# High and low parts of q and k made by ScalarE and GpSimd instead of GpSimd and VectorE

## The chip, the cores and the metric

The kernel runs on one core of a Trainium2 chip. The metric is the device time of one execution in microseconds (us); the time before is the median of three runs. The engines are TensorE (PE, with its weight loads as PEld), VectorE (DVE), ScalarE (ACT), GpSimd (POOL) and SyncE (SP), whose queue issues the DMAs of this kernel. Each engine works through its own queue in order.

## The reference

One layer of a decoder trunk on 2048 rows of width 1024. Cut to what matters here:

```
h = rms(x) * (1 + scale1(c)) + shift1(c)
u = h @ W_in                       # q, k, v of 8 FoX heads x 64 and of 4 differential heads x (2 x 64)
q = rms(q) * gain_q ; k = rms(k) * gain_k          # per head of 64
FoX:   p = softmax(q k^T / 8 + cumulated log forget gates), causal ; out = p v
diff:  p = softmax(q1 k1^T / 8 + alibi) - lam * softmax(q2 k2^T / 8 + alibi), causal ; out = rms(p v)
x = x + gate1(c) * (concat(FoX, diff) @ W_out)
x = x + gate2(c) * SwiGLU(rms(x) * (1 + scale2(c)) + shift2(c))
```

## The kernel before

All large products are made of fp16 operands that are split in two: a high part (the value rounded to fp16) and a low part (the value minus its high part). A product is then three passes of PE: high by high, high by low, low by high.

The work of the attention half comes in eight groups (four differential, four FoX); a group has 128 columns each of q, k and v. For a group g the in-projection `inproj_pair` (L418) runs over the 16 blocks of 128 rows in eight pairs, so 64 pairs in all. For each block `project` (L424) makes 24 matmuls (L437) into the bank "ip", of which there is one; ScalarE copies q and k out of it (L438) and makes the high part of v (L442), VectorE makes the low part of v (line 443, shown in the trace at the helper's line L144). Then, once for each pair, `split` (L447) squares q and k (L453, ScalarE), sums and takes an inverse root (L455 to L458, and L129 to L135 of the helper), multiplies q and k by it (L459, VectorE, 128x512), multiplies q by the gains (L461, GpSimd, 128x256), and makes the high and the low part of q (a = 0) and of k (a = 1) at L467 and L468, each 128x256. `turn` (L471) has SyncE issue two transposing DMAs of the result (L474) and, after every second pair, four copies (L479, L480) that put it where the score matmuls read it.

The attention walks over units: one unit is 128 keys against up to 512 queries. `scores` (L569) makes two or three matmuls (L579, L580, L582) into one of two banks "st"; ScalarE takes the exponential (L585) and rounds it to the high part (L590); GpSimd makes the low part (L593), with the same operation and types as L468. `weigh` (L596) uses both parts, three units later (PVLAG = 3), in matmuls L607, L608 and L609; L609 is the one that reads the low part. Ahead of a group of units `max_part` (L534) makes the scores once more for the row maxima, into one of three banks "mx" (L546), and VectorE reduces them (L548, L550); `max_row` (L552) gathers the maxima (L555, VectorE; L558, PE; L559, ScalarE). `finish` (L611) scales the outputs (L617 to L639).

The order of the work: `run` (L715) interleaves lists of steps by their weights. The attention of group g runs beside the in-projection of group g + 1 (80% of it; the rest runs in the first units of the group itself), beside the loading and splitting of the next group's weights (`stage_w`, L302), and beside slower side work: the sums of the conditioning over w_ada (`ada_items`, L784, with VectorE's L194, groups 0 to 3), the decay sums (`decay`, group 2), and the scaling of W_out (L821 and L834 on GpSimd, groups 4 and 5). SyncE's queue holds the transposes L474 together with the loads of w_in and w_ada (L312, L327, L791), the writes of the outputs (L666) and others. Which instruction stands where in each engine's queue is settled when the program is built, by a planner that goes by a model of the instructions' times (the last lines of `kernel`). The in-projection is over at about 1375 us; the output projection and the SwiGLU that follow have neither of the two lines.

Of the kernel before, what the change touches and what calls it, by code (L numbers as in the profile page):

```python
# [13 lines left out]
AF = mybir.ActivationFunctionType  # L14
ALU = mybir.AluOpType
# [40 lines left out]
def trunk(ctx, tc, t):  # L56
# [6 lines left out]
    V, A, G, T = nc.vector, nc.scalar, nc.gpsimd, nc.tensor  # L63
# [3 lines left out]
    def bank(tag, dt=F32):  # L67
        n = 512 if dt == F32 else 1024
        return ps.tile([P, n], dt, tag=tag, bufs=PSB[tag], name=f"ps_{tag}")

    def small(n, tag, bufs=3, dt=F32):
        return tiny.tile([P, n], dt, tag=tag, bufs=bufs, name=f"t_{tag}")
# [53 lines left out]
    def rsqrt(v, out, n):  # L126

        l = small(n, f"rl{n}")
        A.activation(l, v, AF.Ln, bias=0.0, scale=1.0)  # L129
        y = small(n, f"ry{n}")  # L130
        A.activation(y, l, AF.Exp, bias=0.0, scale=-0.5)
        q = small(n, f"rq{n}")
        V.scalar_tensor_tensor(out=q, in0=y, scalar=-0.5, in1=y, op0=ALU.mult, op1=ALU.mult)
        V.tensor_tensor(out=q, in0=q, in1=v, op=ALU.mult)
        V.scalar_tensor_tensor(out=out, in0=q, scalar=1.5, in1=y, op0=ALU.add, op1=ALU.mult)  # L135
# [7 lines left out]
    def sub_scaled(out, in_, s, hi):  # L143
        V.scalar_tensor_tensor(out=out, in0=in_, scalar=s, in1=hi, op0=ALU.mult, op1=ALU.subtract)  # L144
# [73 lines left out]
    def next_u():  # L218
        turn["u"] ^= 1
        return uh[:, turn["u"], :]  # L220

    def next_hl():
        turn["h"] ^= 1
        return uh[:, 2 + turn["h"], :].bitcast(F16)
# [124 lines left out]
    def whalf(g, h):  # L349
        return wbuf[:, (2 * g + h) % 3].rearrange("p (k s n) -> p k s n", k=4, s=2)  # L350
# [56 lines left out]
    def xx(mt):  # L407

        return mt[:, 0:2].rearrange("p c n -> p (c n)").rearrange("p (b a n) -> p b a n", b=NB, a=2)

    def vviews(kind, vt):

        if kind == "fox":
            v4 = vt.rearrange("p b (h n) -> p b h n", h=2)
            return v4, HD
        return vt.rearrange("p b (h n) -> p b h n", h=1), 2 * HD

    def inproj_pair(g, res, b0):  # L418

        kind, i = GROUPS[g]  # L420
        N = 392 if g == 0 else 384
        st = {}

        def project(b):  # L424
            if b == 0:
                st["u"] = next_u().rearrange("p (a b n) -> p a b n", a=2, b=2)
            info = res["info"]
            w4 = [whalf(g, h) for h in range(2)]
            blk = b0 + b
            h4 = hts[blk // 4].bitcast(F16).rearrange("p (k s n) -> p k s n", k=KT, s=2)  # L430
            c = (blk % 4) * P
            pt = bank("ip" if g or blk >= 4 * FIRST else PTAGS[blk % len(PTAGS)])
            terms = [(k, n) for k in range(KT) for n in ((0, 0), (0, 1), (1, 0))]
            if g == 0 and blk == 0:
                terms.sort(key=lambda x: x[1])
            for i, (k, (hs, ws)) in enumerate(terms):
                T.matmul(pt[:, 0:N], lhsT=h4[:, k, hs, c : c + P], rhs=w4[k // 4][:, k % 4, ws, 0:N], start=(i == 0), stop=(i == len(terms) - 1))  # L437
            A.activation(st["u"][:, :, b, :], pt[:, 0 : 2 * P].rearrange("p (a n) -> p a n", a=2), AF.Copy, bias=0.0, scale=1.0)  # L438
            v4, W = vviews(kind, res["vt"])
            vs = pt[:, 2 * P : 3 * P].rearrange("p (h n) -> p h n", n=W)  # L440
            hi, lo = v4[:, blk, :, 0:W], v4[:, blk, :, W + 2 : 2 * W + 2]
            A.activation(hi, vs, AF.Copy, bias=0.0, scale=info["dv"])  # L442
            sub_scaled(lo, vs, info["dv"], hi)
            if g == 0:
                V.scalar_tensor_tensor(out=fgl[:, blk * 8 : blk * 8 + 8], in0=pt[:, 384:392], scalar=info["df"], in1=bfr, op0=ALU.mult, op1=ALU.add)

        def split():  # L447
            info, maps = res["info"], res["maps"]
            u = st["u"]
            uf = u.rearrange("p a b n -> p (a b n)")  # L450
            u8 = u.rearrange("p a b (m d) -> p (a b m) d", m=2)
            sq = sqs
            A.activation(sq, uf, AF.Square, bias=0.0, scale=1.0)  # L453
            ss = small(8, "ss")
            V.tensor_reduce(out=ss, in_=sq.rearrange("p (a d) -> p a d", d=HD), op=ALU.add, axis=AX.X)  # L455
            V.scalar_tensor_tensor(out=ss, in0=ss, scalar=1.0 / HD, in1=info["eps8"], op0=ALU.mult, op1=ALU.add)
            r = small(8, "r8")
            rsqrt(ss, r, 8)  # L458
            V.tensor_tensor(out=u8, in0=u8, in1=r.unsqueeze(2).broadcast_to([P, 8, HD]), op=ALU.mult)  # L459
            u4 = u8[:, 0:4]  # L460
            G.tensor_tensor(out=u4, in0=u4, in1=gains[kind].unsqueeze(1).broadcast_to([P, 4, HD]), op=ALU.mult)  # L461
            hl = next_hl().rearrange("p (m b a n) -> p a b m n", m=2, b=2, a=2)
            u3 = u.rearrange("p a b (m d) -> p a b m d", m=2)
            for a in range(2):
                hi = hl[:, a, :, :, 0:HD] if a == 0 else hl[:, a, :, :, HD:P]
                lo = hl[:, a, :, :, HD:P] if a == 0 else hl[:, a, :, :, 0:HD]
                G.tensor_scalar(out=hi, in0=u3[:, a], scalar1=1.0, scalar2=0.0, op0=ALU.mult, op1=ALU.add)  # L467
                V.tensor_tensor(out=lo, in0=u3[:, a], in1=hi, op=ALU.subtract)  # L468
            st["hl"] = hl.rearrange("p a b m n -> p m (b a n)")

        def turn():  # L471
            maps, hl = res["maps"], st["hl"]
            for m in range(2):
                nc.sync.dma_start(xx(maps[m])[:, b0 : b0 + 2].rearrange("p b a n -> p (b a) n"), hl[:, m], transpose=True)  # L474
            if b0 % 4 == 2:
                c0 = (b0 - 2) * P
                for m in range(2):
                    x4 = xx(maps[m])[:, b0 - 2 : b0 + 2]
                    nc.sync.dma_start(maps[m][0:HD, 2, c0 : c0 + QC].rearrange("p (b n) -> p b n", b=4), x4[0:HD, :, 0])  # L479
                    nc.sync.dma_start(maps[m][0:HD, 3, c0 : c0 + QC].rearrange("p (b n) -> p b n", b=4), x4[HD:P, :, 1])  # L480

        return [(1, lambda: project(0)), (1, lambda: project(1)), (0.2, split)], (0.1, turn)

    def decay():
# [820 lines left out]
```

## Time and profile before

| | |
|---|---|
| median of three runs | 2968.4 us (2966.42 to 2976.47) |
| profiled execution, device time | 2964.29 us |
| its span from first to last instruction | 2962.2 us |
| PE busy | 2726.8 us, 92% |
| VectorE busy | 2212.0 us, 75% |
| ScalarE busy | 1410.4 us, 48% |
| GpSimd busy | 1590.5 us, 54% |

Read the table as averages over stages that differ: the in-projection with its attention fills the time up to about 1450 us, the output projection and the SwiGLU the rest. The device time is 2.1 us over the span, for what lies around the first and the last instruction. Below, "waited for" names the instruction that released a waiting one; an engine's idle time costs something only if PE comes to wait for it.

### The profile page before, as it was taken

What the parts mean: (1) busy time and instruction counts of PE and PEld (TensorE: products, weight loads), DVE (VectorE), ACT (ScalarE), POOL (GpSimd) and SP (SyncE); (2) the same over time, 40 slices, a digit from 0 to 9 for tenths busy, and PEclk for the clock granted to TensorE, in tenths of its full rate; (3) what the DMA queues carried; (4) which work ended last, traced back from release to release, by engine and by line L of the source; (5) the groups of instructions that cost most, each with busy time, mean ns of one, the idle gap of its engine ahead of it and who ended that gap; (6) DMA issues with size and microseconds to landing.
All of it is one profiled execution on the core that took longest, in us unless ns stands there. A gap on an engine that the chain in (4) does not pass through costs nothing. (4 is left out here: it accounts for less than half of the span.)

```text
span 2962.2 us, 49590 instructions
## 1 busy us (share of the span) xinstructions
PE 2726.8 (92%) x18902; PEld 1478.2 (50%) x18902; DVE 2212.0 (75%) x4205; ACT 1410.4 (48%) x2597; POOL 1590.5 (54%) x1392
## 2 busy tenths in 40 slices
PE   4899989889898998999989898989989999999998
PEld 3465656556565555665444343434434444444443
DVE  7887786967868687757744887777878688787775
ACT  4566666656666676876552432223322232233231
POOL 3465556655567687765552645544555445444440
PEclk9899999999999999999999999989999999999999
DMA  6322231312223133124776223222234511111101
GB/s 230 80 79 56 62 76 37 84 48 65 70 53 94 46 97 107 44 62 139 182 188 217 86 65 100 65 85 82 89 100 156 171 58 57 57 48 66 57 22 57
DMA packets 269903, 261.93 MB, mean 88 GB/s; under 512 B 204376, under 2 KB 221144, under 8 KB 263904
## 3 DMA queue, kind: packets, MB, share of 16 engines
q1 hardware_dynamic: 269664, 258.75, 29.9%
q8 instruction: 148, 2.42, 0.3%
q14 instruction: 91, 0.75, 0.1%
HBM read 173.55 MB, written 36.91 MB: 71 GB/s over the span
## 5 line engine op out<-in xcount | busy, mean ns | idle before, releaser
L593 POOL TENSOR_TENSOR pxs<-pxs 128x512 f16<-128x512 f32 (+3 forms) x640 | 686.7, 1088 | 344.9 <-ACT pxs L590 180.7
L437 PE MATMUL ps_ip<-wbuf,ht 128*128 128x384 f16 (+1 forms) x2952 | 565.8, 334 | 21.8 <-DVE vts L144 11.0
L1091 PEld LDWEIGHTS <-mt 128*128 128x128 f16 x3696 | 361.1, 98 | 445.8 <-issue 18.4
L1149 PE MATMUL ps_mx<-wide,ht 128*128 128x512 f16 x2112 | 505.1, 382 | 24.2 <-DVE mt L1153 12.1
L585 ACT ACTIVATE pxs<-ps_st,cells 128x512 f32<-128x512 f32 (+3 forms) x640 | 390.9, 620 | 242.8 <-PE ps_st L580 102.6
L1038 POOL TENSOR_TENSOR pxm<-vts 128x512 f32<-128x512 f32 x220 | 296.8, 1376 | 335.2 <-DMA vts<-in_w_gu_dram 308.2
L437 PEld LDWEIGHTS <-ht 128*128 128x128 f16 x3072 | 296.7, 100 | 254.9 <-issue 61.4
L1091 PE MATMUL ps_st<-ht,mt 128*128 128x512 f16 x1584 | 382.1, 384 | 8.4 <-DVE pxm L1099 3.5
L1091 PE MATMUL ps_pv<-ht,mt 128*128 128x512 f16 x1584 | 379.1, 379 | 0.0
L590 ACT ACTIVATE pxs<-pxs 128x512 f16<-128x512 f32 (+3 forms) x640 | 350.9, 565 | 10.1
L1149 PEld LDWEIGHTS <-ht 128*128 128x128 f16 x2112 | 206.5, 99 | 281.1 <-issue 27.9
L607 PE MATMUL ps_pv<-vts,pxs 128*128 128x129 f16 (+1 forms) x2176 | 340.0, 206 | 6.1 <-DVE os L626 6.0
L608 PE MATMUL ps_pv<-vts,pxs 128*128 128x128 f16 (+1 forms) x2176 | 342.3, 208 | 0.0
L609 PE MATMUL ps_pv<-vts,pxs 128*128 128x129 f16 (+1 forms) x2176 | 325.4, 206 | 17.1 <-POOL pxs L593 16.4
L1153 DVE SCALAR_TENSOR_TENSOR mt<-ps_mx,t_ai,mt 128x512 f32<-128x512 f32 x352 | 256.3, 742 | 65.4 <-PE ps_mx L1149 65.0
L548 DVE TENSOR_REDUCE t_mxc<-ps_mx 128x1 f32<-128x512 f32 x384 | 255.6, 680 | 64.0 <-PE ps_mx L546 63.0
L546 PE MATMUL ps_mx<-mt 71*128 71x512 f16 (+7 forms) x640 | 199.7, 351 | 52.5 <-DVE t_mxc L548 42.3
L609 PEld LDWEIGHTS <-pxs 128*128 128x128 f16 x2176 | 206.3, 98 | 64.8 <-POOL pxs L593 32.6
L607 PEld LDWEIGHTS <-pxs 128*128 128x128 f16 x2176 | 207.1, 97 | 53.2 <-ACT pxs L585 4.4
L579 PE MATMUL ps_st<-mt 67*128 67x512 f16 (+7 forms) x640 | 223.6, 350 | 6.6 <-ACT pxs L585 6.3
L608 PEld LDWEIGHTS <-pxs 128*128 128x128 f16 x2176 | 207.1, 97 | 37.5 <-issue 8.4
L580 PE MATMUL ps_st<-mt 128*128 128x512 f16 (+3 forms) x640 | 223.4, 349 | 0.0
(266 smaller groups left out, 4119.9 us busy)
## 6 DMA issues: line engine op xcount, KB each, us to landing
vts<-in_w_gu_dram SPq DMA_DIRECT2D x44, 1024.0 KB
stg<-in_w_down_dram SPq DMA_DIRECT2D x44, 512.0 KB
stg<-in_w_ada_dram SPq DMA_DIRECT2D x32, 512.0 KB
stg<-in_w_in_dram SPq DMA_DIRECT2D x24, 512.0 KB
mt<-in_w_ada_dram SPq DMA_DIRECT2D x16, 512.0 KB
mt<-mt SPq DMA_DIRECT2D x128, 64.0 KB
mixed<-os SPq DMA_DIRECT2D x32, 256.0 KB
stg<-in_w_out_dram SPq DMA_DIRECT2D x16, 512.0 KB
```

Of the source, the lines that this page charges most:

```text
L437: T.matmul(pt[:, 0:N], lhsT=h4[:, k, hs, c : c + P], rhs=w4[k // 4][:, k % 4, ws, 0:N], start=(i == 0), stop=(i == len(terms) - 1))
L548: V.tensor_reduce(out=mx[:, 4 * j + n : 4 * j + n + 1], in_=b[:, 0:w], op=ALU.max, axis=AX.X)
L585: A.activation(p32[:, c0:QC], b[:, c0:QC], AF.Exp, bias=pshift, scale=1.0)
L590: A.activation(ph[:, c0:QC], p32[:, c0:QC], AF.Copy, bias=0.0, scale=1.0)
L593: (V if hilo[1] == "V" else G).tensor_tensor(out=pl[:, c0:QC], in0=p32[:, c0:QC], in1=ph[:, c0:QC], op=ALU.subtract)
L607: T.matmul(pv[:, jj, :], lhsT=lhs_h, rhs=v4[:, kb, h, 0 : W + 1], start=first, stop=False, skip_group_check=True)
L608: T.matmul(pv[:, jj, 0:W], lhsT=lhs_h, rhs=v4[:, kb, h, W + 2 : 2 * W + 2], start=False, stop=False, skip_group_check=True)
L609: T.matmul(pv[:, jj, :], lhsT=lhs_l, rhs=v4[:, kb, h, 0 : W + 1], start=False, stop=end, skip_group_check=True)
L1038: G.tensor_tensor(out=sums[:, k * 512 : (k + 1) * 512], in0=raw[:, a * 512 : (a + 1) * 512], in1=raw[:, b * 512 : (b + 1) * 512], op=op)
L1091: T.matmul(b.rearrange("p (b n) -> p b n", b=4), lhsT=aw[w][:, APOS[i] * 4 + k, ws, :], rhs=cb[:, :, 2 * k + hb, :], start=(fresh and k == ...
L1149: T.matmul(b, lhsT=aT[:, th, as_, f, j * P : (j + 1) * P], rhs=dnb[:, (2 * q + f) % 4, ws, n * 512 : (n + 1) * 512], start=(f == 0 and z = ...
L1153: V.scalar_tensor_tensor(out=xs, in0=b, scalar=sets[q]["ai"], in1=xs, op0=ALU.mult, op1=ALU.add)
```

## The change

The high parts (L467) go from GpSimd's tensor_scalar to ScalarE's activation (Copy, scale 1), and the low parts (L468) go from VectorE's tensor_tensor to GpSimd's. Shapes, types and buffers are the same, and there are 128 of each: two for each of 64 pairs.

```
@@ -464,8 +464,8 @@
             for a in range(2):
                 hi = hl[:, a, :, :, 0:HD] if a == 0 else hl[:, a, :, :, HD:P]
                 lo = hl[:, a, :, :, HD:P] if a == 0 else hl[:, a, :, :, 0:HD]
-                G.tensor_scalar(out=hi, in0=u3[:, a], scalar1=1.0, scalar2=0.0, op0=ALU.mult, op1=ALU.add)
-                V.tensor_tensor(out=lo, in0=u3[:, a], in1=hi, op=ALU.subtract)
+                A.activation(hi, u3[:, a], AF.Copy, bias=0.0, scale=1.0)
+                G.tensor_tensor(out=lo, in0=u3[:, a], in1=hi, op=ALU.subtract)
             st["hl"] = hl.rearrange("p a b m n -> p m (b a n)")
```

## Rows read from the trace of the kernel before

**Rows 1.** Head of the page: the span and the engines' busy time.
```profile
span 2962.2 us, 49590 instructions
...
PE 2726.8 (92%) x18902; PEld 1478.2 (50%) x18902; DVE 2212.0 (75%) x4205; ACT 1410.4 (48%) x2597; POOL 1590.5 (54%) x1392
```

**Rows 2.** Busy time by stretch (first row: the columns).
```profile
core 0: us, PE busy (x) PEld busy (x) DVE busy (x) ACT busy (x) POOL busy (x), PEclk, DMA share, GB/s
44.00:150.00 106.00, 85.81 (x524) 52.05 (x523) 79.61 (x239) 65.77 (x195) 52.77 (x55) 0.92 0.25 67
150.00:900.00 750.00, 689.57 (x6272) 459.22 (x6270) 569.90 (x1360) 470.14 (x984) 453.27 (x480) 0.99 0.25 63
900.00:1200.00 300.00, 273.64 (x2863) 169.39 (x2862) 233.98 (x527) 208.18 (x434) 224.72 (x224) 0.98 0.31 83
1200.00:1375.00 175.00, 167.07 (x1780) 103.98 (x1778) 119.81 (x273) 129.35 (x266) 116.31 (x129) 0.98 0.30 82
```

**Rows 3.** Waits of PE, 150 to 1375 us: total, times, longest.
```profile
PE ps_mx L546 <- DVE t_mxc L548: 40.8, 39, 5.3
PE ps_pv L609 <- POOL pxs L593: 14.1, 17, 3.4
PE ps_mx L558 <- DVE t_mrow L555: 12.3, 15, 1.8
PE ps_ip L437 <- DVE vts L144: 11.0, 15, 1.8
PE ps_pv L607 <- DVE os L626: 6.0, 5, 1.2
...
PE ps_st L579 <- ACT pxs L585: 3.3, 5, 1.4
```

**Rows 4.** Groups by line and shape: busy us, mean ns | idle before.
```profile
L593 POOL TENSOR_TENSOR pxs<-pxs 128x512 f16<-128x512 f32 x448 | 548.8, 1237 | 255.7 <-ACT pxs L590 139.2 <-issue 61.5 <-PE ps_pv L609 16.7
...
L468 DVE TENSOR_TENSOR uh<-uh 128x256 f16<-128x256 f32 x128 | 112.1, 892 | 40.8 <-POOL uh L467 40.6
...
L467 POOL TENSOR_SCALAR uh<-uh 128x256 f16<-128x256 f32 x128 | 54.8, 439 | 0.0
...
L593 POOL TENSOR_TENSOR pxs<-pxs 128x256 f16<-128x256 f32 x64 | 49.6, 774 | 34.2 <-PE ps_pv L609 14.2 <-ACT pxs L590 9.2 <-PE ps_st L582 3.0
...
L590 ACT ACTIVATE pxs<-pxs 128x256 f16<-128x256 f32 x64 | 26.7, 417 | 1.0
```

**Rows 5.** Timeline of DVE around 620 us: start, us, instruction [idle before].
```profile
619.04 1.93 DVE L194 SCALAR_TENSOR_TENSOR stg<-stg,cells 128x1024 f32<-128x1024 f32 x1 [1.82 <-DMA stg<-in_w_ada_dram]
620.89 2.66 DVE L468 TENSOR_TENSOR uh<-uh 128x256 f16<-128x256 f32 x2
623.47 0.68 DVE L548 TENSOR_REDUCE t_mxc<-ps_mx 128x1 f32<-128x512 f32 x1
```

**Rows 6.** Timeline of POOL, the same moment.
```profile
620.09 3.18 POOL L593 TENSOR_TENSOR pxs<-pxs 128x512 f16<-128x512 f32 x2 [0.21 <-ACT pxs L590]
```

**Rows 7.** Timeline of PE, the same moment.
```profile
624.20 0.59 PE L546 MATMUL ps_mx<-mt 67*128 67x512 f16 x1 [5.27 <-DVE t_mxc L548]
```

**Rows 8.** Timeline of PE: first and last of the 29 waits counted.
```profile
163.61 0.32 PE L546 MATMUL ps_mx<-mt 67*128 67x384 f16 x1 [0.43 <-DVE t_mxc L550]
...
1374.59 0.38 PE L546 MATMUL ps_mx<-mt 71*128 71x512 f16 x1 [0.52 <-DVE t_mxc L548]
```

**Rows 9.** A wait of POOL, 150 to 1375 us.
```profile
POOL uh L461 <- DVE uh L459: 44.1, 37, 2.9
```

**Rows 10.** A wait of DVE, 150 to 1375 us.
```profile
DVE stg L194 <- DMA stg<-in_w_ada_dram: 37.0, 21, 5.1
```

**Rows 11.** Line L479 by itself: who waited for its DMAs (us, times).
```profile
  PEld L546: 2.1, 1
...
  PE ps_mx L546: 1.6, 1
```

More of the change, by code (lines that the diff above doesn't have):

```diff
@@ L466, in split @@
                 lo = hl[:, a, :, :, HD:P] if a == 0 else hl[:, a, :, :, 0:HD]
-                G.tensor_scalar(out=hi, in0=u3[:, a], scalar1=1.0, scalar2=0.0, op0=ALU.mult, op1=ALU.add)
-                V.tensor_tensor(out=lo, in0=u3[:, a], in1=hi, op=ALU.subtract)
+                A.activation(hi, u3[:, a], AF.Copy, bias=0.0, scale=1.0)
+                G.tensor_tensor(out=lo, in0=u3[:, a], in1=hi, op=ALU.subtract)
             st["hl"] = hl.rearrange("p a b m n -> p m (b a n)")
```

## The prediction

> **What bounds it now.** I read the page first. PE is busy for 92% of the span, the next engine, VectorE, for 75% [rows 1]. So time is won or lost where PE stands idle, and only in the stretch that holds the two lines, up to about 1375 us; no later instruction changes.
>
> Second, busy time by stretch [rows 2]. From 150 to 1375 us, 1225 us, PE is busy for 689.57 + 273.64 + 167.07 = 1130.3 us, so idle for 94.7 us: all that can be won here. VectorE is busy for 923.7 us (75%), ScalarE for 807.7 (66%), GpSimd for 794.3 (65%). GpSimd is not even: from 900 to 1200 us it has 224.72 of 300 us, 75%. Between 44 and 150 us PE has 85.81 of 106 us.
>
> Third, whom PE waits for in these 1225 us [rows 3]. VectorE leads: the next row-maximum matmul has no free bank, since VectorE has not reduced the last one (40.8 us), the maxima are not gathered (12.3), the low part of v is not out of the one "ip" bank (11.0), outputs are not scaled (6.0). Together 70.1 us of 94.7. GpSimd's low part of the exponentials costs 14.1, ScalarE 3.3. The change takes work from the engine that PE waits for most and hands it to the two that it hardly waits for.
>
> Fourth, the two lines themselves [rows 4]. L468 takes VectorE 112.1 us in 128 instructions of 892 ns, and VectorE stands idle for 40.6 us more before them, waiting for GpSimd's L467, as it can do nothing that is queued behind. One moment shows how this reaches PE: at 620.89 us two L468 take 2.66 us [rows 5] while two L593 on GpSimd take 3.18 us instead of twice 1.237 [rows 4, 6], and only then comes the reduction at 623.47 [rows 5] for which PE has been idle for 5.27 us [rows 7]. Part of that wait is older: the load of w_ada that VectorE waited for just before (1.82 us [rows 5]), which the change leaves.
>
> **The change, part by part.** The sum is made against the profiled execution (2964.3 us with what lies around its span); the median of the runs shown, 2968.4, is 4.1 us above it, and I add that at the end.
>
> *VectorE loses L468.* Off it go 112.1 us of work and 40.6 us of waiting. On the path lies only what PE feels of them. I went through VectorE's timeline before each wait of PE for VectorE of 0.3 us or more in the 1225 us: 29 waits, 35.3 us in all, have an L468 within the 5 us before their end the first and the last of them: [rows 8]. Ten others (12.8 us) follow a VectorE that stood idle for w_ada, like the 37.0 us of [rows 10]; the rest have other work before them. If each of the 29 shrinks by as much as L468 and its wait took in those 5 us, 28.8 us go. What is late next is the reduction itself or another VectorE instruction queued with it, so I take two thirds: -19 us. Bounds: 0 (all of it taken by the next in line) and -35.3.
>
> *GpSimd trades the high part for the low part.* It loses 128 times 439 ns and gains 128 instructions of the form of the L593 row at 128x256, 774 ns: 128 x 0.335 = +42.9 us of work over the whole in-projection [rows 4]. This lifts it from 65% to 68% in the 1225 us and to about 78% between 900 and 1200. The cover is its idle time; where that is gone, L593 comes late and PE waits at L609. Against it stands what GpSimd gets back where it no longer collides with L468 (0.7 us in the one place of [rows 5, 6]). I take +6 us, somewhat under half of the 14.1 that PE waits for it now [rows 3]; bounds 0 and +20, half of the added work.
>
> The notes on this chip speak against this step. The Trainium skill, "GPSIMD Engine Reference" (section 4.1, Engine selection), says that elementwise work belongs on VectorE, GpSimd being about twice as slow with two inputs. By that the low parts alone would take about 1.8 us on GpSimd where VectorE took 0.9, an estimate from that page and L468's row, and +6 would become more than +20. The rows disagree: 774 ns for the same operation on GpSimd is below the 892 ns that VectorE took beside it [rows 4].
>
> *ScalarE gains the high part.* 128 instructions of the form of the L590 row at 128x256, 417 ns: +53.4 us of work [rows 4], 66% to 70%. The wait moves too: ScalarE now stands in its queue until GpSimd has multiplied q by its gains, and GpSimd itself stands for VectorE before that, 37 times, 44.1 us [rows 9]. Queued behind the waiting instruction are the exponentials (L585) and the copies out of the one "ip" bank (L438, L442), and PE waits for both. The cover is ScalarE's 417 us of idle time and the three units by which PE's use of an exponential lags. PE waits for it 3.3 us now [rows 3]; I take +4. Bounds: 0, and +26, where one pair in four shows in full (worked out under the rivals).
>
> *SyncE's transposes L474* wait for GpSimd's last low part instead of VectorE's. After the gains the chain was two L467 and one L468, 2 x 0.439 + 0.892 = 1.77 us; now it is one high part and two low parts, 0.417 + 2 x 0.774 = 1.97 us [rows 4]. So 128 transposes, the copies L479 and L480 and the loads queued behind them move by 0.2 us, and by a little more or less with each queue. I cost this at nothing: PE and its weight loads wait for the L479 copies for 3.7 us in the whole run [rows 11], because a pair is done long before its scores are due. Without that cover it is 64 x 0.2 = 13 us. The loads of w_ada behind them could come later or earlier; by a few us of the 37.0 in [rows 10] I let this count for the range, not for the sum.
>
> *The start, 44 to 150 us*, has 6 of the 64 pairs and the densest work of VectorE (79.61 of 106 us [rows 2]), and PE is idle for 20.2 us. I take -2 us; bounds -5 and +3.
>
> Sum: -19 + 6 + 4 + 0 - 2 = -11. 2964.3 - 11 = 2953.3, and on the scale of the median 2957.4; I say 2957.
>
> A measurement of this kernel can tell about 0.3%, 8.9 us, from no change; below 2959.5 counts as faster, above 2977.3 as slower.
>
> **Rivals.** (A is the forecast: -9 to -28, 2940 to 2959.)
>
> B, *the next in line.* The 29 waits hold a reduction, an eviction or a weight split as well as L468; if these are the true pace, PE gains about 10 us, and GpSimd's and ScalarE's added work (96 us together) gives 10 back: 2968. For it: in many of the 29, PE waits under 1 us, about one reduction (0.68 us [rows 5]). Against it: VectorE's load falls from 75% to about 67%, and its waiting goes as well.
>
> C, *ScalarE's queue stands still*: slower. Place: the high part of q, ahead of L585, L438 and L442. Price: the wait that GpSimd has now, 44.1 / 37 = 1.19 us [rows 9], passed on to ScalarE, plus its own 0.417 us: 1.61 us for each pair that PE feels in full. The other terms give -19 + 6 - 2 = -15, so from 9 or 10 of the 64 pairs on the gain is gone, and from 15 on it is slower than can be told from no change. With 16 pairs, one in four, it is +26 - 15 = +11: 2979. For it: the planner's model sets the queue's order and misjudges GpSimd, as the 37 waits show. Against it: ScalarE is idle for a third of the time, and PE hardly waits for it today.
>
> D, *GpSimd becomes the bound*, as it would by the page's rule above. Mechanism: between 900 and 1200 us, and wherever L593 already runs back to back, half of the 42.9 us of added work shows at L609: -19 + 21 + 4 - 2 = +4, 2972. For it: the 14.1 us and the 75%. Against it: 774 against 892 ns, and collisions that vanish.
>
> **How the numbers follow.** A 0.48, B 0.22, C 0.22, D 0.08. A is faster; B is no change; C is slower; of D three quarters are no change and a quarter slower: faster 0.48, same 0.28, slower 0.24. The range has to reach from most of A to most of C. Below, it takes in two thirds of the way to the full 35.3 us (2936); above, C with a few more pairs (2981).
>
> **What would show it.** L468 should stand on GpSimd at about 0.7 to 0.8 us and L467 on ScalarE at about 0.42. VectorE's busy time should fall by about 112 us, and the waits L546 for L548 and L437 for L144 should shrink from 40.8 and 11.0 to some 28 and 8 in the same stretch; PE's idle time before 1375 us should fall by about as much as the run's time. GpSimd's row L609 for L593 should rise from 14.1 to about 20, ScalarE's from 3.3 to about 7. I am wrong if the waits for VectorE stay above 60 us together (B), if L579 or L437 come to wait for ScalarE for over 20 us (C), if L609 waits for GpSimd for over 30 (D), or if the time changes after 1375 us, where none of the changed lines run.

## The result, and the profile after

The changed kernel takes 2936.7 us (median of four runs, 2927.6 to 2939.5) against 2968.7 before: 0.9881 of the time, 95% interval 0.9864 to 0.9898. A later set of runs gave 2933.9 us and 0.9884 (0.9862 to 0.9907). The forecast was 2957 us, faster by 11; the change is worth 32 to 36 us, three times that. The direction was right, the size was not; 2936.7 lies at the fast edge of the stated range (2936 to 2981).

The head of the page after (span, then busy time), to be read against [rows 1]:

```profile
span 2937.7 us, 49384 instructions
...
PE 2728.9 (93%) x18902; PEld 1479.9 (50%) x18902; DVE 2111.3 (72%) x4077; ACT 1441.2 (49%) x2725; POOL 1609.5 (55%) x1392
```

The span is 24.5 us shorter and PE's busy time is the same, so PE stood idle for 26.6 us less (2962.2 - 2726.8 = 235.4 before, 208.8 now). VectorE lost 100.7 us of work, ScalarE gained 30.8 and GpSimd 19.0 net.

Busy time by stretch after, to be read against [rows 2] (same columns):

```profile
44.00:150.00 106.00, 86.40 (x499) 50.78 (x498) 71.40 (x222) 66.05 (x197) 55.04 (x53) 0.89 0.23 65
150.00:900.00 750.00, 700.03 (x6389) 468.81 (x6388) 526.33 (x1318) 497.39 (x1076) 476.28 (x487) 0.99 0.26 65
900.00:1200.00 300.00, 282.03 (x2929) 174.52 (x2928) 216.39 (x515) 219.78 (x472) 232.27 (x232) 0.99 0.35 83
1200.00:1375.00 175.00, 168.53 (x1774) 102.71 (x1772) 100.91 (x245) 134.32 (x285) 119.55 (x125) 0.99 0.34 93
```

From 150 to 1375 us PE is busy for 700.03 + 282.03 + 168.53 = 1150.6 of 1225 us, against 1130.3 before: idle for 74.4 us in place of 94.7, while it is already further on in the work. Between 900 and 1200 us GpSimd is at 232.27 of 300 us, 77%, as forecast. The start was not won: PE is busy for 86.40 us of 106 against 85.81, but with fewer instructions (499 for 524) at a lower granted clock (0.89 for 0.92).

PE's waits in the same 1225 us after, to be read against [rows 3]:

```profile
PE ps_mx L558 <- DVE t_mrow L555: 15.7, 11, 2.5
PE ps_ip L437 <- DVE vts L144: 13.5, 12, 2.9
PE ps_mx L546 <- DVE t_mxc L548: 13.1, 19, 1.6
PE ps_st L579 <- ACT pxs L585: 10.2, 18, 1.8
PE ps_pv L609 <- POOL pxs L593: 8.1, 15, 1.0
...
PE ps_pv L607 <- DVE os L626: 3.1, 2, 1.5
```

The wait for the row maxima (L546 for L548) fell from 40.8 us to 13.1, more than the 28 that was forecast. The wait for GpSimd (L609) fell too, from 14.1 to 8.1, where the forecast had it rise to 20. ScalarE (L579) rose from 3.3 to 10.2, more than forecast. A second trace of the changed kernel (e13 below) has 11.2, 7.0 and 8.4 us in these three rows.

The two lines after, to be read against [rows 4], then what ScalarE now waits for ahead of L467 and GpSimd's own wait for VectorE (both from 150 to 1375 us):

```profile
L468 POOL TENSOR_TENSOR uh<-uh 128x256 f16<-128x256 f32 x128 | 88.5, 698 | 1.5 <-ACT uh L467 1.0 <-PE ps_pv L609 0.4
...
L467 ACT ACTIVATE uh<-uh 128x256 f16<-128x256 f32 x128 | 52.8, 415 | 88.5 <-DVE uh L459 79.3 <-POOL uh L461 7.9 <-DVE t_rq L133 0.9
```

```profile
ACT uh L467 <- DVE uh L459: 72.0, 48, 4.7
...
ACT uh L467 <- POOL uh L461: 5.0, 9, 2.3
```

```profile
POOL uh L461 <- DVE uh L459: 51.2, 34, 4.9
```

L468 on GpSimd takes 698 ns and waits for almost nothing; the high part on ScalarE takes 415 ns. Both are as priced. But ScalarE now stands idle for 77 us in its queue ahead of L467, nearly all of it for VectorE's L459. The prediction had the right place for this wait and too small a price: GpSimd's wait of [rows 9] (44.1 us) is still there, 51.2 us now, and ScalarE's comes on top.

Where on the way the time was won, by the first and last start of a line (before, then after): the in-projection's matmuls, and the last product of the SwiGLU.

```profile
L437 PE MATMUL ps_ip<-wbuf,ht x2952: 322/326/534, 43.7 to 1355.6; 128*128 128x384 f16 x179, 128*128 128x392 f16 x18
```

```profile
L437 PE MATMUL ps_ip<-wbuf,ht x2952: 322/326/534, 43.7 to 1327.8; 128*128 128x384 f16 x179, 128*128 128x392 f16 x18
```

```profile
L1149 PE MATMUL ps_mx<-wide,ht x2112: 376/379/634, 1682.6 to 2958.0; 128*128 128x512 f16 x192
```

```profile
L1149 PE MATMUL ps_mx<-wide,ht x2112: 376/379/634, 1662.3 to 2933.6; 128*128 128x512 f16 x192
```

The last in-projection matmul starts 27.8 us earlier (1327.8 for 1355.6). 20.3 us of that are left when the last stage begins (1662.3 for 1682.6), and 24.4 at its end. So most of the gain is made before the last product, and some 4 us in it, where none of the changed lines run; the prediction named a change of time there as a sign of being wrong. Below, traces are parted at the first L1149: 1682.6 us up to it and 1279.6 from it to the end of the span before, 1662.3 and 1275.4 after.

### The profile page after: what moved, and what is told of

Same layout as the page of the kernel before. It is cut to its first block, busy times and chain, and to the rows that moved or that the text cites. A ratio compares the mean times of both kernels' runs of the same rounds, so it can differ in the third digit from the quotient of the medians.

```text
span 2937.7 us, 49384 instructions
## 1 busy us (share of the span) xinstructions
PE 2728.9 (93%) x18902; PEld 1479.9 (50%) x18902; DVE 2111.3 (72%) x4077; ACT 1441.2 (49%) x2725; POOL 1609.5 (55%) x1392
## 4 chain that ended last, share of the span: by engine, by line
PE 52%; DVE 21%; DMA 12%; POOL 6%; ACT 6%; issue 4%; SPq 0%; POOLq 0%; DVEq 0%; ACTq 0%
PE ps_mx L1149 10%; PE ps_ip L437 10%; PE ps_st L1091 7%; PE ps_pv L1091 6%; DMA stg<-in_w_ada_dram 3%; PE ps_ip L934 3%; DMA stg<-stg 2%; PE ps_mx L1091 2%; PE ps_st L579 2%; DVE t_mxc L548 2%; PE ps_st L580 2%; PE ps_pv L609 2%; PE ps_mx L546 2%; PE ps_pv L608 2%; PE ps_pv L607 2%
## 5 line engine op out<-in xcount | busy, mean ns | idle before, releaser
L1149 PE MATMUL ps_mx<-wide,ht 128*128 128x512 f16 x2112 | 505.4, 382 | 11.5 <-ACT ht L139 5.6
L1149 PEld LDWEIGHTS <-ht 128*128 128x128 f16 x2112 | 206.3, 98 | 266.7 <-issue 16.9
L609 PE MATMUL ps_pv<-vts,pxs 128*128 128x129 f16 (+1 forms) x2176 | 325.6, 207 | 9.8 <-POOL pxs L593 8.9
L548 DVE TENSOR_REDUCE t_mxc<-ps_mx 128x1 f32<-128x512 f32 x384 | 256.9, 682 | 93.8 <-PE ps_mx L546 92.0
L579 PE MATMUL ps_st<-mt 67*128 67x512 f16 (+7 forms) x640 | 223.8, 350 | 10.4 <-ACT pxs L585 10.2
L609 PEld LDWEIGHTS <-pxs 128*128 128x128 f16 x2176 | 206.8, 99 | 50.0 <-POOL pxs L593 24.3
L608 PEld LDWEIGHTS <-pxs 128*128 128x128 f16 x2176 | 208.0, 97 | 35.3 <-issue 4.1
L546 PE MATMUL ps_mx<-mt 71*128 71x512 f16 (+7 forms) x640 | 197.3, 350 | 19.6 <-DVE t_mxc L548 13.1
```

Source lines behind the costliest of these rows:

```text
L548: V.tensor_reduce(out=mx[:, 4 * j + n : 4 * j + n + 1], in_=b[:, 0:w], op=ALU.max, axis=AX.X)
L579: T.matmul(b[:, c0:QC], lhsT=K2[0:K, kb * P : (kb + 1) * P], rhs=QA[0:K, q0:q1], start=True, stop=False, skip_group_check=True)
L608: T.matmul(pv[:, jj, 0:W], lhsT=lhs_h, rhs=v4[:, kb, h, W + 2 : 2 * W + 2], start=False, stop=False, skip_group_check=True)
L609: T.matmul(pv[:, jj, :], lhsT=lhs_l, rhs=v4[:, kb, h, 0 : W + 1], start=False, stop=end, skip_group_check=True)
L1149: T.matmul(b, lhsT=aT[:, th, as_, f, j * P : (j + 1) * P], rhs=dnb[:, (2 * q + f) % 4, ws, n * 512 : (n + 1) * 512], start=(f == 0 and z = ...
```

## The experiments

Two theories stood at the start. A: VectorE's load is what counts; whatever leaves VectorE in this stage lets PE run on. B: the planner's order is what counts. The planner writes every queue from a model of the instructions' times, and with a lighter VectorE it wrote another order for all of them; for PE's queue, of 18902 matmuls and as many weight loads, a line-by-line comparison of the two listings shows 69013 lines taken out or put in. C, a side theory, was that GpSimd's relief from the high parts counts. Each run has its own comparison with the kernel before on the same chip, so ratios are compared rather than medians where they are close. Rows of waits are those from 150 to 1375 us throughout; traces are of one execution each.

### One half of the change at a time

```
e1:   A.activation(hi, u3[:, a], AF.Copy, bias=0.0, scale=1.0)     # high part as in the change
      V.tensor_tensor(out=lo, in0=u3[:, a], in1=hi, op=ALU.subtract)
e2:   G.tensor_scalar(out=hi, in0=u3[:, a], scalar1=1.0, scalar2=0.0, op0=ALU.mult, op1=ALU.add)
      G.tensor_tensor(out=lo, in0=u3[:, a], in1=hi, op=ALU.subtract)  # low part as in the change
```

> High parts on ScalarE, low parts left on VectorE. Theory A (VectorE's load is what counts): the 112 us of low parts stay on VectorE, only the 40.6 us that it stood waiting for GpSimd change hands, so between a quarter and a half of the gain: 2951 to 2961 us against 2968. Theory B (the planner's new order of TensorE's queue is what counts): the order changes here too, so nearly the whole gain or none may show, and it need not lie between the two kernels. Theory C (GpSimd's relief from the high parts is what counts): the full gain, about 2937, and L609 waits for GpSimd for under 8 us.

> Low parts on GpSimd, high parts left on GpSimd, which has both: +128 x 0.77 = 99 us of work there instead of +43. Theory A: VectorE is as free as in the changed kernel, so most of the gain, 2935 to 2950, and the wait of L546 for L548 at about 13 us. Theory C: the gain is gone or turned round, 2965 to 2990, with L609's wait for GpSimd well over 14 us. Theory B gives no value.

Measured: the high part alone gives 2954.6 us, 0.9963 (0.9948 to 0.9977), a third of the gain, in the middle of what theory A expected. The low part alone gives 2925.7 us, 0.9869 (0.9855 to 0.9882): the whole gain and possibly more, with GpSimd doing both. That ends theory C: GpSimd was given 87 us of work and nothing was taken from it. The wait for the row maxima is 23.9 us in this run, where about 13 were expected, and the kernel is no slower for it than the changed one. The group of L468 and PE's waits in the first of these:

```profile
L468 DVE TENSOR_TENSOR uh<-uh 128x256 f16<-128x256 f32 x128 | 87.2, 685 | 24.5 <-ACT uh L467 24.2
```

```profile
PE ps_mx L546 <- DVE t_mxc L548: 22.9, 18, 3.9
PE ps_st L579 <- ACT pxs L585: 14.3, 17, 1.6
```

VectorE still has L468, but for 87.2 us and 24.5 us of waiting in place of 112.1 and 40.8; PE's wait for the row maxima falls to 22.9. PE's wait for ScalarE rises to 14.3, which eats a part of it.

### The order of the queues

```
e3, e4:  with _tile.TileContext(nc, schedule_with_timeline_sim=False) as tc:     # kernel before, changed kernel
e5, e6:  st["hl"] = ...; V.memset(dmy, 0.0)      # dmy: 64 columns, once for each pair; kernel before, changed kernel
```

> The kernel before with the queues' order made by the planner's default mode in place of its simulated timeline; it is the base for the next run. Theory A expects nothing of its time by itself; 2950 to 3100 us.

> The changed kernel with the same default mode of the planner. TensorE's queue then differs from the run before in far fewer places (2937 lines of difference instead of 69013). Theory A: 20 to 40 us faster than that run. Theory B: within 8 us of it.

> The kernel before with one write of 64 zeros by VectorE added to each of the 64 pairs (some 6 to 9 us of VectorE in all), which makes the planner write another order for every queue (61514 lines of difference for TensorE). Theory A: 2962 to 2978 us, the order alone is worth little. Theory B: it could move by 15 us or more either way.

> The changed kernel with the same added writes (10369 lines of difference for TensorE to the changed kernel). Theory A: 2932 to 2948 us. Theory B: it could lose much of the gain, 2950 or more.

Measured: in the planner's default mode both are far slower, 3202.0 (over the 3100 that were expected at most) and 3163.1 us, and the change is worth 39 us there: 1.0796 (1.0771 to 1.0821) against 1.0669 (1.0652 to 1.0687). With the added writes the kernel before stays where it was, 2967.0 us, 0.9997 (0.9986 to 1.0008), though its order is another one, and the changed kernel gives 2930.8 us, 0.9876 (0.9862 to 0.9889). So the gain shows under three different orders, and theory B falls as the main cause. The order isn't without weight, though: in e5's trace the last product begins at 1694.7 us, 12.1 later than before, and from there on it takes 1274.3 us, 5.3 less; its unchanged time is the sum of such parts and of the scatter between executions. PE's waits in the default mode, before and after the change:

```profile
PE ps_mx L546 <- DVE t_mxc L548: 57.3, 39, 4.3
...
PE ps_st L579 <- ACT pxs L585: 17.0, 32, 1.2
```

```profile
PE ps_st L579 <- ACT pxs L585: 41.1, 55, 4.4
PE ps_mx L546 <- DVE t_mxc L548: 40.7, 34, 4.5
```

Both of the forecast's mechanisms stand in these rows side by side: VectorE's relief (57.3 to 40.7) and ScalarE's queue (17.0 to 41.1, the wait of rival C). The kernel is 39 us faster all the same, so VectorE's relief reaches further than this one row.

### More work for one engine

```
e7:   V.tensor_tensor(out=lo, ...); V.tensor_tensor(out=lo, ...)     # kernel before, the low part twice
e8:   G.tensor_tensor(out=lo, ...); G.tensor_tensor(out=lo, ...)     # changed kernel, the low part twice
e11:  A.activation(hi, ...); A.activation(hi, ...)                   # changed kernel, the high part twice
```

> The kernel before with each low part made twice by VectorE: the opposite of the change on VectorE, +112 us of work there and nothing for the others. Theory A: slower by about what the change gained, 2985 to 3010, with the waits of TensorE for VectorE between 150 and 1375 us going from 75 to over 100 us. If VectorE's load had slack: within 8 us of 2968.

> The changed kernel with each low part made twice by GpSimd: +128 x 0.67 = 86 us of work there. The prediction priced 43 us of GpSimd at +6 us, so by it 2945 to 2952 us. If GpSimd has slack for it: 2930 to 2942. If GpSimd's queue is near its limit: over 2960.

> The changed kernel with each high part made twice by ScalarE: +53 us of work there, its waits unchanged. The prediction priced ScalarE's 53 us with its waits at +4, so by it 2937 to 2943 us. If ScalarE's work is dear in this stage, as the 11 us between the changed kernel and the one with both parts on GpSimd hint: 2945 to 2960. If only its waiting is dear: within 5 us of 2937.

Measured: on VectorE the second low part costs 60 us, 3027.2 us, 1.0204 (1.0187 to 1.0221), more than the 3010 that theory A allowed. On GpSimd it costs some 20 us over the changed kernel, 2956.0 us, 0.9962 (0.9948 to 0.9976) for 0.988, between the guesses. On ScalarE the second high part costs some 12 us, 2947.3 us, 0.9923 (0.9908 to 0.9938). For VectorE, its L468 and PE's wait, then the head of the page:

```profile
L468 DVE TENSOR_TENSOR uh<-uh 128x256 f16<-128x256 f32 x256 | 210.1, 849 | 35.6 <-POOL uh L467 35.1
```

```profile
PE ps_mx L546 <- DVE t_mxc L548: 53.2, 38, 5.9
```

```profile
span 3025.8 us, 49738 instructions
...
PE 2755.6 (91%) x18902; PEld 1491.6 (49%) x18902; DVE 2296.3 (76%) x4333; ACT 1406.1 (46%) x2597; POOL 1605.5 (53%) x1392
```

The second low parts are 210.1 - 112.1 = 98 us of VectorE, and 60 of them show: six tenths. All of it comes before the last product, which begins at 1749.4 us for 1682.6; from there on it takes 1276.4 us for 1279.6, and PE's instructions stand there in the same order as before, one for one. Of the 63.6 us by which the span grew, PE was idle for 34.8 (270.2 against 235.4) and its busy time rose by 28.8: the same matmuls took longer. The granted clock (third column from the right) says where; the same stretch in the kernel before stands second:

```profile
750.00:900.00 150.00, 134.02 (x1143) 86.80 (x1141) 104.23 (x238) 88.79 (x177) 88.04 (x88) 0.91 0.21 54
```

```profile
750.00:900.00 150.00, 139.67 (x1318) 93.13 (x1316) 111.73 (x257) 96.49 (x205) 93.66 (x100) 0.99 0.24 64
```

PE had fewer instructions to do in it (1143 against 1318), stood idle more, and was granted 0.91 of the clock on the mean in place of 0.99, that is, it ran for a part of these 150 us at 1.2 GHz in place of 2.4. So idle time of PE cost twice here, by itself and by slower matmuls. The second price is rough: PE's busy time is up to 19 us longer also where PE idled less than before (2745.9 us in e1's trace).

PE's waits in the changed kernel with a second low part on GpSimd (e8), and with a second high part on ScalarE (e11):

```profile
PE ps_st L579 <- ACT pxs L585: 18.6, 23, 3.9
PE ps_mx L546 <- DVE t_mxc L548: 18.4, 19, 3.0
PE ps_pv L609 <- POOL pxs L593: 13.8, 21, 2.0
```

```profile
PE ps_st L579 <- ACT pxs L585: 16.7, 20, 2.1
PE ps_mx L546 <- DVE t_mxc L548: 13.8, 18, 3.0
```

Both show most at ScalarE's L579 (18.6 and 16.7 us for 10.2); a second low part on GpSimd shows less at GpSimd's own L609 (13.8 for 8.1). The row of the maxima rises to 18.4 in e8 and stays at 13.8 in e11. Of e11's 12 us some 6 come before the last product (it begins at 1667.7 us, for 1662.3 and 1661.6 in two traces of the changed kernel).

### The relief by itself

```
e9:   G.tensor_scalar(out=hi, ...)                      # as before
      V.memset(lo, 0.0) if g == 0 and b0 < 4 else None  # in place of the subtraction
e15:  A.activation(hi, ...)                             # as in the change
      V.memset(lo, 0.0) if g == 0 and b0 < 4 else None
```

> The kernel before with the low parts of q and k left out (their place holds zeros from the first two pairs on): VectorE has neither the work nor the wait for GpSimd, and nobody takes them over. This is the relief by itself. The prediction's bound for it is 35 us, so by the prediction no faster than 2930. Theory A with the price that doubling showed (60 us for 98 us of busy time) puts it at 45 to 60 us: 2908 to 2922. If the low parts on GpSimd cost nothing, it equals the run with both parts on GpSimd, about 2926.

> High parts on ScalarE, low parts left out (zeros in their place from the first two pairs on). Against the run with the low parts left out and the high parts on GpSimd (0.984 of the kernel before) it shows ScalarE's price without any low part: 8 to 12 us slower than that, about 2935, if ScalarE's place in the chain costs; equal to it, about 2925, if GpSimd's relief from the high parts makes up for it.

Measured: without the low parts, 2924.8 us, 0.9842 (0.9823 to 0.9862); with the high parts on ScalarE besides, 2941.3 us, 0.9911 (0.9890 to 0.9931). The first is the number that the prediction lacked: taking L468 and its wait from VectorE is worth 1.58%, 47 us (41 to 53 by the interval; the medians of this set differ by 43), if nobody takes them over. In the trace the last product begins at 1656.9 us, 25.7 earlier than before, and from there on it takes 1273.4 us, 6.2 less. PE's waits in it:

```profile
PE ps_mx L546 <- DVE t_mxc L548: 18.0, 21, 3.0
PE ps_mx L558 <- DVE t_mrow L555: 17.8, 14, 2.5
PE ps_ip L437 <- DVE vts L144: 8.4, 6, 2.9
PE ps_pv L609 <- POOL pxs L593: 7.2, 10, 2.2
PE ps_pv L607 <- DVE os L626: 3.4, 4, 1.5
...
PE ps_st L579 <- ACT pxs L585: 1.2, 2, 0.7
```

The four rows of waits for VectorE that the prediction summed to 70.1 us are down to 47.6. L609's wait for GpSimd fell from 14.1 to 7.2 although GpSimd does exactly what it did. That does not show that VectorE's work was behind it: in e7, with more of that work, the row fell as well, to 8.7. What sets it stays open.

The second is slower than the first by 0.7%, 20 us (16 by the medians), where 8 to 12 were expected. The traces don't show this as ScalarE's price: in e15's the last product begins at 1657.1 us, as without it (1656.9), and from there on it takes 1281.8 us for 1273.4. Neither line runs there; PE's instructions stand there in e15 one for one as in the kernel before, in e9 in another order. (e9's traced execution lay 7 us above its median, so as much is not placed.) ScalarE does wait in its own queue in e15, but its trace shows no loss by it:

```profile
ACT uh L467 <- DVE uh L459: 66.6, 43, 3.7
```

### Both parts on GpSimd, beside the change

Edits: none to the changed kernel, and that of e2.

> The changed kernel once more, timed beside the next two so that differences of a few microseconds can be told. About 2936 us if its earlier median holds; 2928 to 2932 if that was at the upper end.

> Both parts on GpSimd once more. If the high parts are dearer on ScalarE than on GpSimd: 8 us or more below the changed kernel of this call. If the earlier 11 us lay in the scatter between calls: within 5 us of it.

Measured side by side: the changed kernel 2933.9 us, 0.9884 (0.9862 to 0.9907), both parts on GpSimd 2925.5 us, 0.9853 (0.9833 to 0.9874). The second beats both kernels: 8.4 us are what the high parts cost more on ScalarE than on GpSimd. The two intervals still touch, but each of the four runs of the second (2922.5 to 2927.5) is below each of the five of the first (2930.0 to 2940.1), and e2 had the same median (2925.7) in another set of runs. In the traces the last product begins at 1650.0 and 1646.1 us with both parts on GpSimd, at 1662.3 and 1661.6 in the changed kernel. The two lines and PE's waits with both on GpSimd (e14):

```profile
L468 POOL TENSOR_TENSOR uh<-uh 128x256 f16<-128x256 f32 x128 | 88.0, 698 | 0.0
...
L467 POOL TENSOR_SCALAR uh<-uh 128x256 f16<-128x256 f32 x128 | 54.5, 438 | 0.0
```

```profile
PE ps_mx L546 <- DVE t_mxc L548: 27.1, 26, 3.3
PE ps_pv L609 <- POOL pxs L593: 10.3, 18, 1.4
...
PE ps_st L579 <- ACT pxs L585: 2.4, 7, 0.7
```

L579's wait for ScalarE is back at 2.4 us (3.3 before the change, 10.2 after it), and L609's for GpSimd is 10.3 although GpSimd has 88 us more than before. Nothing waits ahead of either line: high and low part follow L461 in one queue. The row of the maxima is at 27.1 us, twice that of the slower changed kernel, so rows of waits alone don't price a change. Against e9 (0.9842) the low parts on GpSimd cost 0.1 to 0.3%, and the intervals overlap: that they cost anything isn't shown.

### Two tries further

```
e10:  V.tensor_copy(hi, u3[:, a])                                            # high part on VectorE
      G.tensor_tensor(out=lo, in0=u3[:, a], in1=hi, op=ALU.subtract)
e12:  as e2, and  G.tensor_tensor(out=u8, in0=u8, in1=r..., op=ALU.mult)     # L459 on GpSimd too
```

> High parts on VectorE (a copy to fp16), low parts on GpSimd. ScalarE has nothing of it and VectorE waits for GpSimd's gains only. If the load on VectorE counts, the copies (128 of some 0.3 to 0.9 us, 40 to 110 us) take back a part: 2935 to 2955. If VectorE's waiting is what counts, it is as good as both parts on GpSimd or the changed kernel: 2925 to 2937.

> Both parts on GpSimd, and also the multiplication by the inverse root (L459, 47 us on VectorE, about 90 us on GpSimd). The whole chain from L459 to the low parts is then on one engine. If VectorE's load still counts more than GpSimd's: 2910 to 2922 us. If GpSimd has now become the bound: over 2935, with L609's wait for it over 20 us between 150 and 1300 us.

Measured: the high part on VectorE gives nearly everything back, 2962.2 us, 0.9983 (0.9970 to 0.9996), more than either guess. Its L467:

```profile
L467 DVE CAST uh<-uh 128x256 f16<-128x256 f32 x128 | 73.7, 584 | 17.2 <-POOL uh L461 16.2
```

73.7 + 17.2 = 90.9 us of VectorE cost 36 us against both parts on GpSimd, four tenths. Not all of that need be VectorE's load: GpSimd now waits for VectorE's high part, 12.7 us in all ahead of L468. L459 on GpSimd as well gives 2939.9 us, 0.9901 (0.9885 to 0.9916): worse than without by 14 us. Its L459 and PE's wait for GpSimd:

```profile
L459 POOL TENSOR_TENSOR uh<-uh,t_r 128x512 f32<-128x512 f32 x64 | 71.2, 1112 | 83.0 <-DVE t_r L135 49.0 <-DVE t_rl L622 19.3 <-DVE t_p2a L115 5.0
```

```profile
PE ps_pv L609 <- POOL pxs L593: 10.7, 20, 1.3
```

The gain is given back here, but not where it was looked for: L609 waits for GpSimd no longer than before (10.7 us). In the traces most of the loss lies where L459 doesn't run: the last product begins at 1654.2 us for 1650.0 in e14, and from there on it takes 1287.4 us for 1275.4. GpSimd stands idle for 83.0 us ahead of L459, 49.0 of them for VectorE's inverse root, with the exponentials' low parts queued behind. A chain that starts with a wait was put into the queue that had none; that this wait cost the 4 us ahead of the last product is argued, not shown.

## Why the prediction was wrong

**The step that failed** is the first term of the sum, "VectorE loses L468", taken at two thirds: -19 us. The run that has this relief alone (e9) is 43 to 47 us faster. Beside it failed the premise that "no later instruction changes", by which everything behind the two lines stood at nothing. The mechanism was right: VectorE's time is what counts in this stage, as e9 and the runs that add work to VectorE (e7 above all) show. Three things make the difference between 19 and 43 to 47.

- It took two thirds, since the next instruction on VectorE would be late. In e9's trace the last product begins 25.7 us earlier, and the four rows of waits fell by 22.5 us (70.1 to 47.6). The gathering (L558) rose by 5.5, so the next in line was late by little. Up to the last product the trace puts the term at -26, inside its bound of -35.3.
- What comes behind the two lines was put at nothing. The last product is 6 us shorter in e9, and 4 and 9 us shorter in the two traces of the changed kernel (1275.4 and 1270.5 us for 1279.6). The planner wrote its instructions in another order. In the four traces that have PE's old order there (before, e7, e11, e15) this product takes 1276.4 to 1281.8 us, in the three that have the changed kernel's (its own two and e10) 1270.5 to 1276.1. So part of the gain seems to go with the order of a stage that the change doesn't touch. How large a part is rough, since one and the same order differs by 5 us between executions, and no run tested the order there by itself.
- It looked at one profiled execution. That execution (2964.3 us) lay 4 us under the median, e9's (2932.2) 7 us above its own (so the two traces show 32 of the 43 us), and that of the changed kernel (2939.5) was the longest of its four. So the traces of before and after differ by 24.8 us where the medians differ by 32 (and by 36 in the later set). The clock has no part in those 24.8: PE's busy time is the same in both, and the 26.6 us of idle time are the whole difference.

**GpSimd's term**, +6 us, was not far off: by e14 and e9 its low parts cost 0.1 to 0.3%, 3 to 8 us, which can't be told from nothing. Its sign at L609 was wrong (8.1 us where 20 were forecast). The rule of the Trainium skill that was weighed there ("GPSIMD Engine Reference", section 4.1) would have priced the step at more than +20; the run with both parts on GpSimd, the fastest of all complete kernels here, disagrees. In this stage VectorE took 892 ns for the operation on the mean and GpSimd 698. The shortest ones, 398 ns on VectorE and 658 on GpSimd, do go the way of the rule.

**ScalarE's term**, +4 us, was too small. Against GpSimd the high parts on ScalarE cost 8.4 us with the low parts on GpSimd (e13, e14); without any low parts the traces show none ahead of the last product (e9, e15). The bound of +26 held. The wait was named, but 44.1 us were expected of it and 77 came. How much of the price is the 53 us of work and how much the wait is not settled: doubling the work alone cost 12 us (e11), half of it in the last product.

**SyncE's transposes**: nothing, as said; PE's weight loads wait for the L479 copies for 0.2 us in the changed kernel, against [rows 11]. **The start**: nothing was won where -2 was said.

The runs give -47 for VectorE (e9), +3 for the low parts on GpSimd (e14 for e9) and +9 for the high parts on ScalarE (e13 for e14), -35 in all. That is no check, as each step is measured from the one before it and the last is the change itself. By way of e15 the same -35 would be -47, +20 and -8. The order of the queues moves single traces by some 10 us in a stage (e5, e15), so terms of this size aren't told apart.

**The rivals.** B (the next in line) fell with e9 and e7. C was right about the place and the wait, wrong about who wins: PE feels it, and VectorE's relief is several times as large. D fell with e14. That the order of the queues might carry the gain was no rival in the prediction; as the main cause it is ruled out (e3 to e6), as a part of some 10 us it is not. It also goes some way to say why the changed kernel is 7 us faster than the same kernel without any low parts (e13 against e15): in the traces e15 begins the last product 4.5 us earlier (1657.1 for 1661.6), as work left out should, and takes 11 us more for it (1281.8 for 1270.5), with PE in the old order.

## What to carry to other kernels

When an engine is the one that the bound engine waits for most, price its microseconds by doubling or leaving out the suspected instruction in a run, not by counting the waits that name it: here three to six tenths of each microsecond of work and waiting taken from or given to VectorE showed in the time (47 us for 152.9 in e9, 36 for 90.9 in e10, 60 for 98 in e7). Where a planner rewrites all queues, look in the trace at which stage the time moved in: up to some 10 us of these differences lie in a stage that none of the edits touch. Move such work into a queue that already holds the instruction before it in the chain: with both parts behind L461 on GpSimd nothing waited, while ScalarE's queue took over a wait of 77 us.

## What the runs showed of the hardware

GpSimd and VectorE hold each other up, and a small instruction can lose most. At the longest wait of PE for GpSimd in the kernel before (PE first, then GpSimd, then VectorE):

```profile
1137.28 0.24 PE L609 MATMUL ps_pv<-vts,pxs 128*128 128x65 f16 x1 [3.43 <-POOL pxs L593]
```

```profile
1129.54 2.35 POOL L834 TENSOR_TENSOR stg<-stg,grep 128x1024 f32<-128x1024 f32 x1 [0.48 <-DMA stg<-in_w_out_dram]
...
1134.03 1.70 POOL L461 TENSOR_TENSOR uh<-uh,gg_fox 128x256 f32<-128x256 f32 x1 [1.03 <-DVE uh L459]
```

```profile
1129.62 2.29 DVE L133 SCALAR_TENSOR_TENSOR t_rq<-t_ry 128x8 f32<-128x8 f32 x1 [0.44 <-ACT t_ry L131]
...
1133.87 1.28 DVE L144 SCALAR_TENSOR_TENSOR stg<-stg,cells 128x1024 f16<-128x1024 f32 x1
```

At 1129.62 us a 128x8 instruction of VectorE, which takes its tile from SBUF twice, as both inputs, and whose line has a median of 164 ns over the run, took 2.29 us: it ended with GpSimd's L834, which had begun just before it (1129.54 + 2.35 = 1131.89). It belongs to the inverse root of a pair, so the whole chain came 2 us late. Then GpSimd's L461, 0.73 us at the median, took 1.70 us beside VectorE's L144 of 1.28 us; the low part of the exponentials was queued behind it, and PE waited 3.43 us for that at L609. So a wait that is put down to GpSimd began on VectorE, and one on VectorE began on GpSimd. No L468 is in this chain. The Trainium skill, "SBUF — State Buffer" (Terms, "shared port pair"), says that the two engines share a pair of ports which one holds for a whole instruction while the other is blocked; these rows agree. That VectorE's L468 went from a least time of 398 ns to 2329 ns, and GpSimd's from 658 to 1651 ns, is probably the same thing from both sides; the mean on GpSimd (698 ns) lies near its least, that on VectorE (892 ns) far above.

Not expected either: PE's granted clock fell where PE was idle more (0.91 against 0.99 in the 150 us shown of e7); over that run PE's idle time grew by 34.8 us and its busy time by 28.8 for the same matmuls.
